# Half of the next block's transposed inputs loaded into the free columns of the row scales' buffer

## The chip, the cores and the metric

One core of a Trainium2 chip runs the whole program; 7 other cores of the chip are not used. The metric is the time of one execution on the device, in microseconds (us). Engines: TensorE (PE; its weight loads are PEld), VectorE (DVE), ScalarE (ACT), GpSimd (POOL); SyncE (SP) and POOL issue the DMAs.

## What is computed

One inference step of a one-layer streaming encoder: 2048 prompt frames and 64 sample frames of width 1024, all float32. Cut to what matters here:

```python
hn   = rms(x) * (1 + sc1) + sh1            # adaLN-modulated pre-norm
proj = hn @ w_in                           # q, f, iv, og (HGRN2), xr, gr (RG-LRU)
...
y = concat([o_hg, o_rg]) @ w_out
x = x + g1 * y
hn2 = rms(x) * (1 + sc2) + sh2
x = x + g2 * (square(relu(hn2 @ w_up)) @ w_down)   # D_FF = 4096
y_out = rms(x) * final_gain
```

## The kernel before

The prompt is cut into four blocks of 512 frames (`BLK`); the last block also carries the 64 sample frames. A block goes through the pre-norm (`phase_A`), the two mixers, the output projection (`phase_O`) and the MLP. The MLP runs over 8 groups `g` of 512 hidden columns. `phase_U(g)` multiplies by `w_up` (4 weight units, 96 matmuls of 512 columns) and squares the relu. `phase_W(g - 1)` multiplies the group before by `w_down`: 7 products instead of 8 (a Strassen-like scheme), 84 matmuls. In block 0 a plain product, `phase_D0` with 96 matmuls, stands in its place. After group 7's `phase_U` come `phase_W(6)` and `phase_W(7)`, and then the next block's projections. The stretch around the last three of these is called a **seam** here: seam 1 is from block 0 to 1, seam 2 from 1 to 2, seam 3 from 2 to 3.

Every weight is float32 and is used as a high part and a rest. `split_raw` casts a loaded `raw` tile on ACT (L244) and subtracts on DVE (L245) into a `wt` tile; the pool `wp` has 6 of them. `phase_W` first makes its 7 weights in `down_units`: two of the four loaded `w_down` units go to `raw` buffers (L250, 3 of them), two to row buffers (L1032 and L1033), then DVE combines them with four subtractions (L1036) and splits seven tiles. The products accumulate in PSUM, and DVE adds each to its accumulator (L1086; L1068 in block 0). For `phase_W(g)` itself the operand sums of `phase_U(g)` are made by `sums_of`: splits (L964 on ACT, L965 on DVE) and four additions (L970 to L974). 

The next block's pre-norm is begun inside the MLP of the block before. `phase_A1` (in group 5) computes the row scales. `phase_A` (in group 7) spreads them over 128 partitions with TensorE (`ps_rs`, L529), copies them to the first 512 columns of a buffer `hd_a` of 2560 columns (L531), and loads the block's input once more, transposed, in four tiles of 128 x 1024 (L501, `in_x_t`). Each tile gives two column groups: DVE multiplies by scale (L538), ACT writes the high part (L539), DVE the rest (L540): 16 DVE instructions a block. For the last block `phase_A` first norms the 64 sample frames over a buffer `hd_a` of their own (`norm_T`, L390 to L419).

Buffers of a tag are shared by all that asks for that tag:

- `xa`: 2 buffers. The first two tiles of the transposed input; the `x2r` tiles of the final phase, `phase_E` (L1180).
- `row`: 2 buffers of 1028 columns. **The last two tiles of the transposed input**, two of the four `w_down` units of every `phase_W`, the row vectors `final_gain` and `gscr` (L351), and earlier in a block temporaries of the RG-LRU.
- `hd`: 2 buffers of 2560 columns: `hd_u` of `phase_U`, `hd_a` of `phase_A`, `hd_h` of the heads.

The order of the work on each engine is made by the tile scheduler from priorities (`sec(block, rank)`) and from its own estimate of when buffers come free. Each engine, and SP's DMA queue too, then works its list off in order: what waits holds all that stands behind it.

```python
x = rowp.tile([P, 1028], F32, tag="row", name="x_a")[:, :D] if row else xap.tile([P, D], F32, tag="xa", name="x_a")   # L500
...
r12, r22 = (rowp.tile([P, 1028], F32, tag="row", name="raw")[:, :D] for _ in range(2))   # L1031, in down_units
Q.dma_start(r12, w_down[u + 2])   # L1032
```

Of the kernel before, what the change touches and what calls it, by code (L numbers as in the profile page):

```python
# [9 lines left out]
F32 = mybir.dt.float32  # L10
# [9 lines left out]
P = 128  # L20
D = 1024
# [108 lines left out]
def hymba_step(ctx: ExitStack, tc: tile.TileContext, i: dict, o: dict):  # L130
# [18 lines left out]
    def pool(name, bufs, **k):  # L149
        return ctx.enter_context(tc.tile_pool(name=name, bufs=bufs, **k))  # L150
# [8 lines left out]
    xap = pool("xap", 2)  # L159
    rowp = pool("rowp", 2)  # L160
# [216 lines left out]
    def rms_rstd(x, junk, n):  # L377
        ss = smp.tile([P, 8], F32, tag="ss", name="ss")
        S.activation(junk[:n], x[:n], AF.Square, accum_out=ss[:n, 0:1])
        V.tensor_scalar(ss[:n, 0:1], ss[:n, 0:1], 1.0 / D, EPS, op0=ALU.mult, op1=ALU.add)  # L380
        return rsqrt(ss, n, 1)

    def norm_T(xn, hn, XT, t0, n, which, psc, psh):

        hv = hn.rearrange("p (k t) -> p k t", t=P)
        for hf in range(2):
            ps = pax.tile([P, 512], F32, tag="ax", name="ps_T")
            for q in range(4):
                k = hf * 4 + q
                T.transpose(ps[:, q * P:q * P + n], xn[:n, k * P:(k + 1) * P], ident[:n, :n])  # L390
            for q in range(4):
                k = hf * 4 + q
                sc, sh = modc[:, psc, which, k:k + 1], modc[:, psh, which, k:k + 1]
                if q % 2:
                    V.tensor_scalar(hv[:, k, :n], ps[:, q * P:q * P + n], sc, sh, op0=ALU.mult, op1=ALU.add)
                else:
                    S.activation(hv[:, k, :n], ps[:, q * P:q * P + n], AF.Identity, scale=sc, bias=sh)
            ks = slice(hf * 4, hf * 4 + 4)
            S.copy(XT.p[0][:, ks, t0:t0 + n], hv[:, ks, :n])  # L399
            V.tensor_tensor(XT.p[1][:, ks, t0:t0 + n], hv[:, ks, :n], XT.p[0][:, ks, t0:t0 + n].bitcast(F32), op=ALU.subtract)  # L400
            if which:
                XT.pair(ks)
# [50 lines left out]
    for b in range(NB):  # L453
        B = Block()
# [38 lines left out]
    def gate(dma, ins):  # L493
        tc.add_manual_dep(dma.ins, ins.ins.name,
                          mybir.DependencyInfo(mybir.DependencyClass.Sync, mybir.DependencyReason.DATA),
                          reason="late load")


    def x_load(src, n, after, row=False):
        x = rowp.tile([P, 1028], F32, tag="row", name="x_a")[:, :D] if row else xap.tile([P, D], F32, tag="xa", name="x_a")  # L500
        d = Q.dma_start(x[:n], src)  # L501
        if after is not None:
            gate(d, after)
        return x

    def phase_A1(B, after=None):

        ss = smp.tile([P, 8], F32, tag="ss", name="ss_a")
        for t in range(4):
            x = x_load(xp[B.toks[t][4]:B.toks[t][4] + P], P, after)  # L510
            S.activation(x, x, AF.Square, accum_out=ss[:, t:t + 1])
        V.tensor_scalar(ss[:, 0:4], ss[:, 0:4], 1.0 / D, EPS, op0=ALU.mult, op1=ALU.add)
        B.rs = rsqrt(ss, P, 4)

    def phase_A(B, after=None):


        B.XT = Split(xtp, "xt", KD, "XT1")
        if B.last:
            n = LS  # L520
            x = x_load(xs, n, after)
            hd = hdp.tile([P, 2560], F32, tag="hd", name="hd_a")
            rs = rms_rstd(x, hd[:, :D], n)
            V.tensor_scalar(x[:n], x[:n], rs[:n, 0:1], None, op0=ALU.mult)
            norm_T(x, hd[:, 0:D], B.XT, BLK, n, 1, SC1, SH1)
        hd = hdp.tile([P, 2560], F32, tag="hd", name="hd_a")
        ps = pax.tile([P, 512], F32, tag="ax", name="ps_rs")
        for t in range(4):
            T.matmul(ps[:, t * P:(t + 1) * P], lhsT=B.rs[:, t:t + 1].to_broadcast([P, P]), rhs=ident, start=True, stop=True)  # L529
        rb = hd[:, 0:BLK]  # L530
        S.copy(rb, ps)  # L531
        for k2 in range(4):
            x = x_load(i["x_t"][B.b, k2], P, after, k2 > 1).rearrange("p (k t) -> p k t", k=2)
            for kk in range(2):
                k = 2 * k2 + kk
                sc, sh = modc[:, SC1, 0, k:k + 1], modc[:, SH1, 0, k:k + 1]
                hi, lo = (y[:, k, :BLK] for y in B.XT.p)
                V.scalar_tensor_tensor(x[:, kk], x[:, kk], sc, rb, op0=ALU.mult, op1=ALU.mult)  # L538
                S.activation(hi, x[:, kk], AF.Identity, bias=sh)  # L539
                V.scalar_tensor_tensor(lo, x[:, kk], sh, hi.bitcast(F32), op0=ALU.add, op1=ALU.subtract)  # L540
# [686 lines left out]
    if blocks[0].last:  # L1227
        run([ada_first(0)], 99)
        run(ada_s, 99)
        phase_A(blocks[0])  # L1230
    else:
        phase_A0(blocks[0])
# [4 lines left out]
    for B in blocks:  # L1237
# [48 lines left out]
        for g in range(NG):  # L1286
            if B.last and g == NG - 1:
                with sec(b, 177):
                    phase_W(B, g - 1, gts[g - 1])
                with sec(b, 178):  # L1290
                    combine(B)
            with sec(b, 110 + 10 * g):
                gts.append(phase_U(B, g))
            if g == 5 and not B.last:
                with sec(b, 161):
                    phase_A1(blocks[b + 1], B.ulast)
            if g == NG - 1 and not B.last:
                with sec(b, 182):
                    phase_A(blocks[b + 1])
            if g and not (B.last and g == NG - 1):  # L1300
                with sec(b, 115 + 10 * g):
                    (phase_W if b else phase_D0)(B, g - 1, gts[g - 1])
                with sec(b, 116 + 10 * g):
                    if b == 0 and g < 7:
                        run(ada_s, 11)
# [33 lines left out]
```

## Time and profile before

| | |
|---|---|
| median of 3 runs | 2690.6 us (2690.57 to 2698.39) |
| the profiled execution | 2700.03 us; span 2698.3 us, so 1.7 us lie around the span |
| mean granted clock of TensorE | 0.955 of full speed |
| PE busy | 2493.6 us, 92% of the span |
| DVE busy | 1817.2 us, 67% |
| ACT busy | 1043.5 us, 39% |
| POOL busy | 188.0 us, 7% |
| DMA | 397 MB, 147 GB/s on the mean |

A share of the span is a mean over stages with different limits. What the stages at the seams wait for stands in the timeline of instructions: there, "[13.81 <-ACT wt L244]" behind an instruction says that its engine stood idle for 13.81 us before it, and that the cast of line 244 ended the wait.

### The profile page before, as it was taken

To read this page: it belongs to the slowest core of one execution; us is meant where nothing else is said; L and a number is where in the kernel's file an instruction comes from. 1 tells how busy PE (TensorE), PEld (TensorE's weight loads), DVE (VectorE), ACT (ScalarE), POOL (GpSimd) and SP (SyncE) were. 2 spreads that over 40 slices of the span, in tenths; PEclk is the share of its full clock that TensorE was granted. 3 is DMA by queue.
4 is the path that set the end of the run, shared out by engine and by line. 5 is a ranking of instruction groups with operands and counts; after the bars stand their busy time and mean duration, and the time that the engine had idled before them with its cause. 6 is when DMAs were issued, how large, how long until landed. Compare 5 with 4: busy or idle time off the path is not lost.

```text
span 2698.3 us, 34804 instructions
## 1 busy us (share of the span) xinstructions
PE 2493.6 (92%) x13592; PEld 2129.3 (79%) x13592; DVE 1817.2 (67%) x3267; ACT 1043.5 (39%) x1683; POOL 188.0 (7%) x245
## 2 busy tenths in 40 slices
PE   5878899999899999999799989999789998999997
PEld 4866787887797778888587878888579877998976
DVE  7676675766554656878864656778773576568787
ACT  4234152223212446445312436445411624644432
POOL 2311100000011100000001100000010110000000
PEclk8888799999999999999899999999889999999998
DMA  8563555667353542234363442234253643222223
GB/s 332 219 227 132 202 182 187 211 210 242 126 203 124 180 141 78 94 110 156 113 223 125 180 140 79 94 109 153 93 207 110 149 126 129 79 78 92 81 68 109
DMA packets 96420, 397.44 MB, mean 147 GB/s; under 512 B 14432, under 2 KB 16384, under 8 KB 79360
## 3 DMA queue, kind: packets, MB, share of 16 engines
q1 hardware_dynamic: 79696, 274.63, 29.6%
q0 software_dynamic: 16560, 120.59, 12.9%
q8 instruction: 107, 1.75, 0.3%
q14 instruction: 57, 0.47, 0.0%
HBM read 343.77 MB, written 51.41 MB: 146 GB/s over the span
## 4 chain that ended last, share of the span: by engine, by line
PE 70%; DVE 14%; issue 7%; DMA 5%; ACT 3%; POOL 1%; SPq 0%; DVEq 0%; POOLq 0%; ACTq 0%
PE ps_u L1011 24%; PE ps_d L1097 15%; PE ps_in L649 7%; PE ps_vo L767 6%; PE ps_d L1063 6%; PE ps_y L937 3%; DMA raw<-in_w_ada_dram 2%; PE ps_lv L841 2%; DVE wt L245 2%; PE ps_in L634 1%; PE ps_rg L710 1%; DVE ada_acc L333 1%; PE ps_s L1107 1%; PE ps_ada L337 1%; DMA wt<-kept_out 1%
## 5 line engine op out<-in xcount | busy, mean ns | idle before, releaser
L1011 PE MATMUL ps_u<-XT,wt 128*128 128x512 f32 (+2 forms) x4128 | 746.5, 341 | 17.1 <-ACT XT L399 5.9
L1011 PEld LDWEIGHTS ps_u<-XT,wt 128*128 128x128 f32 x4128 | 656.0, 189 | 99.4 <-ACT XT L399 7.1
L245 DVE TENSOR_TENSOR wt<-raw,wt 128x1024 fp32r<-128x1024 f32 x338 | 414.9, 1240 | 237.6 <-ACT wt L244 206.1
L244 ACT CAST wt<-raw 128x1024 fp32r<-128x1024 f32 x357 | 371.4, 1048 | 331.4 <-PE ps_d L1063 93.1
L649 PE MATMUL ps_in<-XT,wt 128*128 128x512 f32 (+1 forms) x1776 | 377.7, 363 | 12.9 <-ACT wt L244 6.6
L649 PEld LDWEIGHTS ps_in<-XT,wt 128*128 128x128 f32 x1776 | 293.0, 191 | 60.3 <-ACT wt L244 8.5
L1097 PE MATMUL ps_d<-wt,gS 128*128 128x512 f32 x1104 | 269.0, 402 | 41.0 <-ACT wt L244 30.7
L1097 PEld LDWEIGHTS ps_d<-wt,gS 128*128 128x128 f32 x1104 | 212.8, 194 | 92.8 <-ACT wt L244 32.3
L937 PE MATMUL ps_y<-wt,mix 128*128 128x512 f32 x800 | 207.1, 413 | 13.6 <-DVE hd_o L942 5.1
L1014 ACT ACTIVATE hd_u<-ps_u 128x512 f32<-128x512 f32 (+2 forms) x172 | 85.2, 498 | 344.3 <-PE ps_u L1011 341.0
L767 PE MATMUL ps_vo<-wt,XT 128*128 128x256 f32 x1600 | 212.6, 289 | 2.6 <-POOL wt L245 1.7
L767 PEld LDWEIGHTS ps_vo<-wt,XT 128*128 128x128 f32 x1600 | 201.0, 195 | 3.9 <-POOL wt L245 1.9
L1097 PE MATMUL ps_d<-wt,gA 128*128 128x512 f32 x828 | 196.9, 390 | 0.2
L937 PEld LDWEIGHTS ps_y<-wt,mix 128*128 128x128 f32 x800 | 154.8, 198 | 53.0 <-DVE hd_o L942 6.4
L1063 PE MATMUL ps_d<-wt,gt 128*128 128x512 f32 x768 | 182.2, 398 | 8.3 <-DVE acc L1068 8.3
L1097 PEld LDWEIGHTS ps_d<-wt,gA 128*128 128x128 f32 x828 | 154.7, 188 | 33.0 <-DVE wt L245 1.0
L1063 PEld LDWEIGHTS ps_d<-wt,gt 128*128 128x128 f32 x768 | 147.9, 193 | 40.1 <-DVE acc L1068 8.7
L1036 DVE TENSOR_TENSOR raw<-raw 128x1024 f32<-128x1024 f32 x92 | 113.4, 1233 | 4.3 <-DMA raw<-in_w_down_dram 2.2
L841 PEld LDWEIGHTS ps_lv<-hd_h 128*128 128x128 f32 x640 | 88.9, 211 | 24.6 <-issue 15.6
L1086 DVE TENSOR_TENSOR acc<-acc,ps_d 128x512 f32<-128x512 f32 x160 | 106.5, 680 | 1.9 <-PE ps_d L1097 0.9
L841 PE MATMUL ps_lv<-hd_h 128*128 128x64 f32 x640 | 92.3, 292 | 14.5 <-DVE hd_h L846 9.0
L1086 DVE TENSOR_TENSOR accM<-accM,ps_d 128x512 f32<-128x512 f32 x120 | 79.7, 681 | 38.5 <-PE ps_d L1097 38.1
(306 smaller groups left out, 2671.1 us busy)
## 6 DMA issues: line engine op xcount, KB each, us to landing
wt<-kept_in POOLq DMA_DIRECT2D x72, 1024.0 KB, 6.8
raw<-in_w_up_dram SPq DMA_DIRECT2D x128, 512.0 KB, 4.3
raw<-in_w_down_dram SPq DMA_DIRECT2D x128, 512.0 KB, 3.5
raw<-in_w_ada_dram SPq DMA_DIRECT2D x80, 512.0 KB, 4.8
wt<-kept_out POOLq DMA_DIRECT2D x24, 1024.0 KB, 5.2
kept_in<-wt POOLq DMA_DIRECT2D x19, 1024.0 KB, 8.8
raw<-in_w_in_dram SPq DMA_DIRECT2D x24, 512.0 KB, 5.3
x_a<-in_x_prompt_dram SPq DMA_DIRECT2D x16, 512.0 KB, 5.3
```

What stands on the lines that cost most here:

```text
L244: S.copy(wt[:, 0], raw)
L245: eng.tensor_tensor(wt[:, 1], raw, wt[:, 0].bitcast(F32), op=ALU.subtract)
L649: T.matmul(ps[:, :pn], lhsT=w[:, a, k], rhs=B.XT.p[x][:, k, p0:p0 + pn], start=(k == 0 and q == 0), stop=(k == KD - 1 and q == 2))
L767: T.matmul(ps[:rows(B.toks[ti]), :256], lhsT=l, rhs=ws[k // 4][:, a, k % 4], start=(q == 0), stop=(q == len(ops) - 1))
L841: T.matmul(ps[:C, c * C // 2:(c + 1) * C // 2].rearrange("p (b h) -> p b h", h=hs), lhsT=KS[:, c * C:c * C + C], rhs=qv[:, c * bc:(c + 1) ...
L937: T.matmul(ps[:rows(B.toks[ti])], lhsT=l, rhs=ws[k - k % 2][:, a, k % 2], start=(q == 0), stop=(q == len(ops) - 1))
L1011: T.matmul(ps[:, :pn], lhsT=w[:, a, k], rhs=B.XT.p[x][:, k, p0:p0 + pn], start=(k == 0 and q == 0), stop=(k == KD - 1 and q == 2))
L1014: S.activation(r, ps[:, :pn], AF.Relu)
L1036: V.tensor_tensor(d, x, y, op=ALU.subtract)
L1063: T.matmul(ps, lhsT=l, rhs=ws[half][c // 2][:, a, c % 2], start=(q == 0), stop=(q == len(ops) - 1))
L1086: return V.tensor_tensor(dst, dst, ps, op=ALU.add)
L1097: T.matmul(ps, lhsT=op[x][y][:, c, t * P:(t + 1) * P], rhs=w[:, a, c], start=(k == 0), stop=(k == len(ops) - 1))
```

## The change

`x_load` takes the buffer as an argument instead of a flag. `phase_A` issues its four loads ahead of the copy of the row scales, and the last two tiles no longer take row buffers: they lie in columns 512 to 1535 and 1536 to 2559 of `hd_a`, whose first 512 columns hold the row scales as before.

```diff
-    def x_load(src, n, after, row=False):
-        x = rowp.tile([P, 1028], F32, tag="row", name="x_a")[:, :D] if row else xap.tile([P, D], F32, tag="xa", name="x_a")
+    def x_load(src, n, after, x=None):
+        if x is None:
+            x = xap.tile([P, D], F32, tag="xa", name="x_a")
         d = Q.dma_start(x[:n], src)
...
         rb = hd[:, 0:BLK]
+        xts = [x_load(i["x_t"][B.b, k2], P, after, hd[:, k2 * D - 1536:k2 * D - 512] if k2 > 1 else None) for k2 in range(4)]
         S.copy(rb, ps)
         for k2 in range(4):
-            x = x_load(i["x_t"][B.b, k2], P, after, k2 > 1).rearrange("p (k t) -> p k t", k=2)
+            x = xts[k2].rearrange("p (k t) -> p k t", k=2)
```

The number and the sizes of all instructions stay the same. Behind line 500 the changed file's lines are 1 higher, behind line 531 2 higher: its L1034 and L1035 are L1032 and L1033 of before, L1038 is L1036, L1088 is L1086, L540 and L542 are L538 and L540.

The list of SP's DMA queue at seam 2, before, from the first transposed loads on (two `x_a` are the tiles of tag `xa`, the next two those of tag `row`; L1032 and L1033 load `w_down` units to row buffers, first for group 6, then for group 7):

```order
L501 DMA x_a<-in_x_t_dram 128x1024 x2
L250 DMA raw<-in_w_up_dram 128x1024
L501 DMA x_a<-in_x_t_dram 128x1024 x2
L250 DMA raw<-in_w_up_dram 128x1024 x2
L250 DMA raw<-in_w_down_dram 128x1024 x3
L1032 DMA raw<-in_w_down_dram 128x1024
L1033 DMA raw<-in_w_down_dram 128x1024
L250 DMA raw<-in_w_down_dram 128x1024
```

and the same place in the change:

```order
L502 DMA x_a<-in_x_t_dram 128x1024 x2
L250 DMA raw<-in_w_up_dram 128x1024
L1034 DMA raw<-in_w_down_dram 128x1024
L1035 DMA raw<-in_w_down_dram 128x1024
L250 DMA raw<-in_w_up_dram 128x1024 x2
L250 DMA raw<-in_w_down_dram 128x1024 x3
L502 DMA hd_a<-in_x_t_dram 128x1024 x2
L250 DMA raw<-in_w_down_dram 128x1024
```

Group 6's two row-buffer loads and the last two transposed tiles have changed places.

The list of DVE at seam 2, before, from the splits during `phase_U(7)` on, through the beginning of `phase_A`'s 16 instructions (the 16 end thirteen rows further on, one row behind the first L1086; the first L1036 of group 6 comes two rows after them):

```order
L245 TENSOR_TENSOR wt<-raw,wt 128x1024 x5
L965 TENSOR_TENSOR gA_9562<-hd_u,gA_9562 128x512
L538 SCALAR_TENSOR_TENSOR x_a<-x_a,modc,hd_a 128x512 x3
L540 SCALAR_TENSOR_TENSOR XT_9587<-x_a,modc,XT_9587 128x512 x2
L965 TENSOR_TENSOR gA_9565<-hd_u,gA_9565 128x512
L540 SCALAR_TENSOR_TENSOR XT_9587<-x_a,modc,XT_9587 128x512
L538 SCALAR_TENSOR_TENSOR x_a<-x_a,modc,hd_a 128x512 x2
```

and in the change:

```order
L245 TENSOR_TENSOR wt<-raw,wt 128x1024 x4
L1038 TENSOR_TENSOR raw<-raw 128x1024
L245 TENSOR_TENSOR wt<-raw,wt 128x1024
L1038 TENSOR_TENSOR raw<-raw 128x1024
L245 TENSOR_TENSOR wt<-raw,wt 128x1024 x2
L967 TENSOR_TENSOR gA_9560<-hd_u,gA_9560 128x512
L1038 TENSOR_TENSOR raw<-raw 128x1024 x2
L245 TENSOR_TENSOR wt<-raw,wt 128x1024 x2
L540 SCALAR_TENSOR_TENSOR x_a<-x_a,modc,hd_a 128x512 x3
L542 SCALAR_TENSOR_TENSOR XT_9585<-x_a,modc,XT_9585 128x512
```

All four subtractions and four more splits of group 6's weights now stand ahead of `phase_A`'s first instruction. Where the 16 instructions end, the change has the last split of group 6 and then the first L1088:

```order
L245 TENSOR_TENSOR wt<-raw,wt 128x1024
L542 SCALAR_TENSOR_TENSOR XT_9585<-hd_a,modc,XT_9585 128x512
L1088 TENSOR_TENSOR accM<-accM,ps_d 128x512 x2
L1088 TENSOR_TENSOR acc<-acc,ps_d 128x512 x3
```

So the first addition from PSUM stands behind all 16 of them, as it stood behind 15 before.

At seam 3 (`hd_a` of L395 is the sample frames' buffer) the change's DVE list reads, from the first subtraction to the first of the 16:

```order
L1038 TENSOR_TENSOR raw<-raw 128x1024
L967 TENSOR_TENSOR gA_14160<-hd_u,gA_14160 128x512
L1038 TENSOR_TENSOR raw<-raw 128x1024
L245 TENSOR_TENSOR wt<-raw,wt 128x1024 x2
L1038 TENSOR_TENSOR raw<-raw 128x1024 x2
L245 TENSOR_TENSOR wt<-raw,wt 128x1024
L395 TENSOR_SCALAR hd_a<-ps_T,modc 128x64 x3
...
L245 TENSOR_TENSOR wt<-raw,wt 128x1024
L967 TENSOR_TENSOR gA_14163<-hd_u,gA_14163 128x512
L400 TENSOR_TENSOR XT_14185<-hd_a,XT_14185 128x4x64
L245 TENSOR_TENSOR wt<-raw,wt 128x1024
L540 SCALAR_TENSOR_TENSOR x_a<-x_a,modc,hd_a 128x512
```

Here nine of group 6's instructions (four subtractions, five splits) have come ahead, where before none of them stood between those rows. At seam 1, where `phase_D0` takes no row buffers, DVE's list is in the same order as before, and SP's two `hd_a` loads stand behind five `w_down` loads and the store of `gscr`, where the two row-buffer tiles stood among the first of those.

## Rows read from the trace of the kernel before

**Rows 1.** The page, chain that ended last: share of the span by engine.

```profile
PE 70%; DVE 14%; issue 7%; DMA 5%; ACT 3%; POOL 1%; SPq 0%; DVEq 0%; POOLq 0%; ACTq 0%
```

**Rows 2.** By stretch, seam 2: length; busy PE, PEld, DVE, ACT, POOL; clock; DMA share, GB/s.

```profile
1280.00:1300.00 20.00, 17.87 (x83) 14.60 (x81) 7.67 (x13) 9.25 (x15) 0.00 (x0) 1.00 0.00 1
1300.00:1320.00 20.00, 8.28 (x25) 6.16 (x26) 18.98 (x26) 6.85 (x9) 0.00 (x0) 0.58 0.23 79
1320.00:1340.00 20.00, 18.53 (x77) 13.81 (x76) 19.52 (x24) 6.77 (x9) 0.53 (x1) 1.00 0.50 171
```

**Rows 3.** Timeline of PE, seam 2: start, us, engine, instruction, [idle before <-releaser].

```profile
1269.58 21.92 PE L1011 MATMUL ps_u<-XT,wt 128*128 128x512 f32 x96
...
1292.15 5.72 PE L1097 MATMUL ps_d<-wt,gA 128*128 128x512 f32 x24
1311.68 12.51 PE L1097 MATMUL ps_d<-wt,gS 128*128 128x512 f32 x42 [13.81 <-ACT wt L244]
...
1356.53 11.04 PE L649 MATMUL ps_in<-XT,wt 128*128 128x512 f32 x48
...
1374.50 1.65 PE L820 MATMUL ps_dg<-hd_h 128*128 128x128 f32 x8 [3.10 <-POOL hd_h L816]
```

**Rows 4.** Timeline of all engines, seam 2.

```profile
1293.31 2.08 DVE L538 SCALAR_TENSOR_TENSOR x_a<-x_a,modc,hd_a 128x512 f32<-128x512 f32 x3 [10.00 <-ACT hd_a L531]
...
1305.66 0.33 SPq L1032 DMA_DIRECT2D raw<-in_w_down_dram  x1
...
1309.32 1.22 DVE L1036 TENSOR_TENSOR raw<-raw 128x1024 f32<-128x1024 f32 x1
...
1310.58 1.04 ACT L244 CAST wt<-raw 128x1024 fp32r<-128x1024 f32 x1 [2.87 <-DVE raw L1036]
```

**Rows 5.** Timeline of SP's queue, ahead of seam 2.

```profile
1250.32 3.96 SPq L501 DMA_DIRECT2D x_a<-in_x_t_dram  x2
```

**Rows 6.** Chain in order of time, seam 2: start, us, what.

```profile
1302.44 0.66 DVE x_a L538
...
1304.36 0.60 DVE hd_u L974
...
1309.41 1.15 DVE raw L1036
```

**Rows 7.** Timeline of all engines, seam 3.

```profile
1902.38 0.34 DVE L395 TENSOR_SCALAR hd_a<-ps_T,modc 128x64 f32<-128x64 f32 x1 [9.16 <-ACT hd_a L397]
1902.90 5.72 PE L1097 MATMUL ps_d<-wt,gA 128*128 128x512 f32 x24
...
1907.20 2.07 DVE L538 SCALAR_TENSOR_TENSOR x_a<-x_a,modc,hd_a 128x512 f32<-128x512 f32 x3
...
1923.12 1.22 DVE L1036 TENSOR_TENSOR raw<-raw 128x1024 f32<-128x1024 f32 x1 [1.03 <-DMA raw<-in_w_down_dram]
...
1925.47 1.65 PE L1097 MATMUL ps_d<-wt,gS 128*128 128x512 f32 x3 [16.86 <-ACT wt L244]
1925.55 1.22 DVE L1036 TENSOR_TENSOR raw<-raw 128x1024 f32<-128x1024 f32 x1 [1.21 <-DMA raw<-in_w_down_dram]
```

**Rows 8.** Timeline of PE, end of seam 3.

```profile
1970.61 9.68 PE L649 MATMUL ps_in<-XT,wt 128*128 128x288 f32 x72
...
1986.60 1.16 PE L820 MATMUL ps_dg<-hd_h 128*128 128x128 f32 x8 [2.36 <-POOL hd_h L816]
1991.03 1.97 PE L841 MATMUL ps_lv<-hd_h 128*128 128x64 f32 x8 [3.27 <-DVE hd_h L817]
```

**Rows 9.** Timelines of SP's queue and of all engines, seam 1.

```profile
678.25 0.29 SPq L346 DMA_DIRECT2D gscr<-grow  x1
...
701.24 0.74 DVE L538 SCALAR_TENSOR_TENSOR x_a<-x_a,modc,hd_a 128x512 f32<-128x512 f32 x1
...
712.51 12.70 PE L1063 MATMUL ps_d<-wt,gt 128*128 128x512 f32 x47 [8.25 <-DVE acc L1068]
```

**Rows 10.** The instructions on `in_x_t`, last line: from issue to landing.

```profile
DMA to landing us min/median/max: 3.5/3.6/5.2
```

## The prediction

> **What bounds the kernel now.** I read the chain of waits first: 70% of it is PE and 14% DVE [rows 1], so time is to be had only where PE stands still, and there it is mostly DVE that ends the wait. Then the busy time by stretch: PE is full in the steady groups and has its holes at the seams. At seam 2 it is busy 8.28 of 20 us, and DVE is then at 18.98 and 19.52 of 20, after only 7.67 in the 20 us before [rows 2]. So the seam is bound by DVE, right behind a stretch in which DVE had little to do.
>
> The timelines say why. A matmul of 512 columns takes 21.92 / 96 = 0.228 us in the steady state, so the 168 of `phase_W(6)` and `phase_W(7)` need 38.3 us; from 1292.15 to the next block's first matmul at 1356.53 they took 64.4 [rows 3]. The first 24 ran, then PE stood 13.81 us for a cast [rows 3], and that cast waited for a subtraction L1036 of `down_units` [rows 4]. The subtraction needs the unit of L1032, which SP issued only at 1305.66 [rows 4], because `phase_A`'s last two tiles had taken both row buffers at 1250 [rows 5] and gave them back only when DVE had used them. Meanwhile DVE had stood idle for 10.00 us ahead of `phase_A` [rows 4]. Seam 3 is alike: 16.86 us of PE, 9.16 us of idle DVE ahead of it, and twice more DVE waited for the late units, 1.03 and 1.21 us [rows 7]; from its first matmul at 1902.90 to the projections at 1970.61 it took 67.7 us [rows 7, 8]. At seam 1 PE waits 8.25 us for an addition that stands behind `phase_A` on DVE [rows 9]; no row buffer plays a part.
>
> **The change, part by part.** Nothing is added or removed: the same 12 loads of 512 KB, the same 48 DVE instructions on operands of the same shape, which I cost at nothing more. What changes is when things may start.
>
> *Seam 1.* Row buffers are free sooner, but DVE's and PE's lists there are the same. The two `hd_a` loads go past five `w_down` loads and the store of `gscr` on SP, which was issued at 678.25; a tile lands in at most 5.2 us [rows 10], well before the 701.24 at which `phase_A` begins [rows 9]. 0 us.
>
> *Seam 2.* SP now issues L1032 and L1033 where the row-buffer tiles stood, at 1250 [rows 5]; they land some 25 us before their use. By the new list DVE does four L1036 and four more L245 ahead of `phase_A`. Each holds DVE 1.15 us (the chain's piece [rows 6]), so 8 x 1.15 = 9.2 us of work goes from a stretch without slack into the 10.00 us of idling. Their buffers allow it: each further `wt` comes free when `phase_U(7)` ends a unit, every 5.5 us. The last of the eight waits for the fourth unit, and its cast (1.04 us [rows 4]) now stands on ACT ahead of the copy of the row scales, so `phase_A` begins at about 1294.3, 1.0 us later. DVE's list behind it ends 9.2 - 1.0 = **8.2 us** sooner, and I take that.
>
> It is not the whole stall, since what PE waits for is next the first L1086. PE can go 30 matmuls with the PSUM it has, then needs an addition, which stands behind 16 x 0.66 (`phase_A`), 6 x 0.60 (`sums_of`) [rows 6] and one split of 1.15: 15.3 us from 1294.3, at 1309.6 instead of the 1311.68 at which PE went on before. So I expect a stall of 10 to 11 us in place of 13.81, with another cause. The bounds: below, only what PE gains by that, 2.1 us and 6 more matmuls done, 1.4: 3.5 us. Above, PE without any wait from 1309.6: 138 x 0.228 = 31.5, ending at 1341.1, 15.4 us sooner. DVE's own sum lies between and DVE was without slack there, so I take 8.2.
>
> *Seam 3.* Nine instructions go ahead (four L1036, five L245): 10.3 us, seven of them into the 9.16 us of idling [rows 7]. DVE's waits for late units, 2.24 us [rows 7], go. Against that, `phase_A` begins later than 1907.20: by two splits less one addition that has gone behind (2.3 - 0.6), and one cast, 1.0, on ACT ahead of the copy: 2.7 us, at 1909.9; the addition gone behind costs 0.6 again. 10.3 + 2.2 - 2.7 - 0.6 = **9.2 us**. The first addition that PE then waits for comes 15 x 0.66 + 5 x 0.60 = 12.9 us on, at 1922.8, against 1925.47. Bounds as above: 2.7 + 1.4 = 4.1 us, and 1922.8 + 31.5 = 1954.3, 16.3 us sooner. Here the `hd_a` loads wait: their columns come free when the sample frames' norm is done, at about 1908.5. With a landing of 3.6 us (5.2 at most) [rows 10] they are there at 1912 to 1914, and DVE comes to the first of them after some 7 us of `phase_A`, at 1917. That cover is 3 us; each us beyond it would hold DVE, and PE with it. What stands right behind these loads on SP, a `w_up` unit of the next block and the first `x2r`, is not wanted at the seam.
>
> *Behind the seams.* The next block's first head waited 3.10 us at seam 2 [rows 3], and 2.36 and 3.27 at seam 3 [rows 8], for DVE work that stood behind `phase_E`'s additions of `x2r`, whose loads land late. In the new list L815 stands ahead of the third of these additions. Bounds 0 and 8.7 us; since parts of that head still stand behind them, I take half, **4 us**.
>
> The sum: 8.2 + 9.2 + 4 = 21.4 us off the profiled execution's 2700.03. That execution is 9.4 us above the median of the runs, 2690.6; against the median the forecast is **2669 us**.
>
> **The rivals.**
>
> *The stall only changes its cause.* DVE's list is shorter, but it then waits for PE here and there, and only the earlier restart is left: 3.5 + 4.1 = 7.6 us, 2683. For it: the first L1086 does stay behind all of `phase_A`. Against: DVE was idle for only 1.5 of the 40 us of the seam in rows 2 (20 - 18.98 and 20 - 19.52), so 9 us less work cannot all turn to idling.
>
> *The whole hole closes.* From the restart on PE runs without a wait: 15.4 + 16.3 + 8.7 = 40.4 us, 2650. Against: all 28 additions and all of `down_units(7)` still stand on DVE in those 31 us. The Trainium skill bears on this ("Perfetto Trace Analysis", Optimization Strategy): it reads gaps that repeat as a sign that too few buffers stop the next tile. By that rule the two largest gaps are the row buffers' alone and go with them; the trace agrees as to their cause, and the busy time of DVE right behind them speaks against their going whole.
>
> *Slower: the clock.* In the 20 us of seam 2's stall the granted clock was 0.58, then 1.00 again [rows 2]; the 42 matmuls behind the stall took 12.51 us where 9.6 would do at 0.228 [rows 3], so such a restart costs 2.9 us now. If PE's idling, now in more and shorter pieces, kept the clock at its lower level (half of full speed) through both `phase_W`, the 138 matmuls of a seam would take 31.5 us more, 63 for two, and the kernel 63 - 21 = 42 us longer: 2732. It turns slower from 94 such matmuls over both seams on. For it: a stall of some 10 us stays at each of the two seams. Against: after the stall of 13.81 us the clock was back at 1.00 in the next 20 us, though PE was busy in only 18.53 of them [rows 2]. The Trainium skill ("TensorE: Matmul & The Clock Gate", HAM oscillation) tells of a kernel whose clock fell anew at every gap and lost 26.7 of 211 us by it; by that rule the gaps that I leave would each cost a warm-up, and the seams' gain would shrink by what it costs. The row of 0.58 agrees that a gap lowers it, the row of 1.00 that one warm-up was enough.
>
> *It does nothing:* the loads of L1032 come early but the casts are held by `wt` tiles, 2691. Against: the list has only as many splits ahead as units of `phase_U(7)` end.
>
> **How the numbers follow.** Chances: the forecast with its bounds 0.72, the changed cause 0.12, the closed hole 0.08, slower by the clock (or by late `hd_a` loads at seam 3) 0.05, nothing 0.03. A measurement of this kernel can tell about 0.3%, 8 us, from no change. Faster by more: the forecast, the closed hole and a third of the changed cause, 0.84. Within it: 0.11. Slower: 0.05. The range leaves out the slower case, the closed hole's far end and the no-effect case: from 2659 (half way between what I take and the upper bounds, 21.4 and 40.4) to 2684 (both lower bounds).
>
> **What would show it.** In the profile of the change: L1034 issued near 1250 and DVE busy with L1038 during `phase_U(7)`; the waits of 13.81 and 16.86 us gone from the cast and a wait of 10 to 13 us for an addition (L1088) in their place; the projections 8 to 9 us sooner behind `ps_rs` at each seam; seam 1 as it was. Wrong if seam 1 moves, if DVE is idle for over 3 us in the 40 us from 1300 on, if `hd_a` loads end a DVE wait, or if the clock stays low behind the stall.

## The result and the profile after

| | before | after |
|---|---|---|
| median, first series | 2691.66 us (4 runs, 2690.57 to 2698.39) | 2676.39 us (4 runs, 2673.15 to 2676.63) |
| ratio, first series | | 0.9937, 95% interval 0.9921 to 0.9954 |
| median, second series | 2696.65 us (11 runs) | 2675.62 us (6 runs) |
| ratio, second series | | 0.9918, 0.9905 to 0.9931 |
| profiled execution | 2700.03 us | 2676.52 us (span 2674.7) |
| mean granted clock | 0.955 | 0.958 |
| PE busy / DVE busy | 2493.6 / 1817.2 us | 2492.6 / 1816.1 us |

It is faster by 0.6 to 0.8%: 15.3 us in the first series, 21.0 in the second (experiment 4). The work over the whole span is the same to about 1 us on PE and DVE; only idle time went.

The chain of waits by engine, on the page of after, is that of [rows 1] but for one point between "issue" and DMA:

```profile
PE 70%; DVE 14%; issue 6%; DMA 6%; ACT 3%; POOL 1%; SPq 0%; DVEq 0%; POOLq 0%; ACTq 0%
```

Seam 2, timeline of PE (start, us, instruction, idle before it and its releaser), which answers to [rows 3]:

```profile
1288.91 1.05 PE L530 MATMUL ps_rs<-ident,rsq 128*128 128x128 f32 x8
1289.72 5.72 PE L1099 MATMUL ps_d<-wt,gA 128*128 128x512 f32 x24
1295.28 1.52 PE L1099 MATMUL ps_d<-wt,gS 128*128 128x512 f32 x6
1307.90 11.49 PE L1099 MATMUL ps_d<-wt,gS 128*128 128x512 f32 x42 [11.10 <-DVE accM L1088]
...
1333.00 7.10 PE L1099 MATMUL ps_d<-wt,gS 128*128 128x512 f32 x30 [1.37 <-DVE acc L1088]
...
1342.66 2.66 PE L651 MATMUL ps_in<-XT,wt 128*128 128x512 f32 x11
```

The wait for a cast is gone, and one of 11.10 us for an addition L1088 stands in its place. From `ps_rs` to the first projection it is now 53.75 us, before 65.19. The timeline of DVE there, against [rows 4]:

```profile
1275.62 1.23 DVE L1038 TENSOR_TENSOR raw<-raw 128x1024 f32<-128x1024 f32 x1
...
1290.67 1.22 DVE L245 TENSOR_TENSOR wt<-raw,wt 128x1024 fp32r<-128x1024 f32 x1 [4.21 <-ACT wt L244]
1291.82 2.07 DVE L540 SCALAR_TENSOR_TENSOR x_a<-x_a,modc,hd_a 128x512 f32<-128x512 f32 x3
...
1307.17 1.27 DVE L1088 TENSOR_TENSOR accM<-accM,ps_d 128x512 f32<-128x512 f32 x2
```

The subtractions of group 6 begin at 1275, in the last `phase_U`, where before they began at 1309. `phase_A` starts at 1291.82, and the first addition at 1307.17, 0.7 us ahead of PE's restart: what PE waits for is that addition, behind all 16 instructions of `phase_A`. SP's queue shows why the subtractions could come early (before: [rows 5] and the L1032 of [rows 4]):

```profile
1248.58 0.33 SPq L1034 DMA_DIRECT2D raw<-in_w_down_dram  x1
1251.53 0.33 SPq L1035 DMA_DIRECT2D raw<-in_w_down_dram  x1
...
1271.85 0.90 SPq L502 DMA_DIRECT2D hd_a<-in_x_t_dram  x2
```

Seam 3, timeline of PE, against [rows 7, 8]: 57.84 us from `ps_rs` to the projections, before 68.63.

```profile
1886.28 1.16 PE L530 MATMUL ps_rs<-ident,rsq 128*128 128x128 f32 x8
...
1907.32 10.74 PE L1099 MATMUL ps_d<-wt,gS 128*128 128x512 f32 x36 [11.69 <-DVE accM L1088]
...
1933.02 8.54 PE L1099 MATMUL ps_d<-wt,gS 128*128 128x512 f32 x30 [2.70 <-DVE acc L1088]
...
1944.12 9.68 PE L651 MATMUL ps_in<-XT,wt 128*128 128x288 f32 x72
...
1960.46 2.08 PE L822 MATMUL ps_dg<-hd_h 128*128 128x128 f32 x8 [2.39 <-POOL hd_h L818]
1962.50 1.97 PE L843 MATMUL ps_lv<-hd_h 128*128 128x64 f32 x8
```

Where did 11.4 and 10.8 us come from? The busy time from `ps_rs` to the first projection tells it (length; busy PE, PEld, DVE, ACT, POOL; clock; DMA). Before, seams 2 and 3:

```profile
1291.34:1356.53 65.19, 46.29 (x178) 35.08 (x176) 60.61 (x80) 22.58 (x29) 2.64 (x5) 0.82 0.46 160
...
1901.98:1970.61 68.63, 46.65 (x179) 35.39 (x178) 62.90 (x86) 24.09 (x35) 1.85 (x4) 0.80 0.40 135
```

and after:

```profile
1288.91:1342.66 53.75, 41.28 (x178) 33.50 (x176) 51.41 (x71) 19.13 (x26) 2.64 (x5) 0.90 0.39 141
...
1886.28:1944.12 57.84, 43.45 (x179) 35.10 (x177) 53.88 (x77) 21.02 (x32) 2.79 (x4) 0.85 0.41 149
```

At seam 2 DVE has 60.61 - 51.41 = 9.2 us less work and 4.58 - 2.34 = 2.2 us less idling; at seam 3, 9.0 and 1.8. DVE's groups of instructions name the 9.2 us. Before, seam 2:

```profile
L245 DVE TENSOR_TENSOR wt<-raw,wt 128x1024 fp32r<-128x1024 f32 x12 | 14.2, 1217 | 0.5 <-ACT wt L244 0.5
...
L1036 DVE TENSOR_TENSOR raw<-raw 128x1024 f32<-128x1024 f32 x8 | 9.7, 1217 | 0.0
...
L1115 DVE TENSOR_TENSOR acc<-acc,accM 128x512 f32<-128x512 f32 x4 | 2.6, 680 | 0.0
...
L1115 DVE TENSOR_TENSOR acc<-acc 128x512 f32<-128x512 f32 x2 | 1.4, 682 | 0.0
```

and after:

```profile
L245 DVE TENSOR_TENSOR wt<-raw,wt 128x1024 fp32r<-128x1024 f32 x9 | 10.8, 1218 | 4.2 <-ACT wt L244 4.2
...
L1038 DVE TENSOR_TENSOR raw<-raw 128x1024 f32<-128x1024 f32 x4 | 4.9, 1218 | 0.0
...
L1117 DVE TENSOR_TENSOR acc<-acc,accM 128x512 f32<-128x512 f32 x3 | 2.1, 685 | 0.0
...
L1117 DVE TENSOR_TENSOR acc<-acc 128x512 f32<-128x512 f32 x1 | 0.7, 683 | 0.0
```

Four subtractions and three splits (8.0 us at 1.15) have left the seam, and two closing additions (L1117, 1.2 us) now lie behind the first projection, since PE's last product is done sooner.

### The profile page after: what moved, and what is told of

It reads as the page before. It is cut to its first block, busy times and chain, and to the rows that moved or that the text cites. A ratio compares the mean times of both kernels' runs of the same rounds, so it can differ in the third digit from the quotient of the medians.

```text
span 2674.7 us, 34794 instructions
## 1 busy us (share of the span) xinstructions
PE 2492.6 (93%) x13592; PEld 2135.7 (80%) x13592; DVE 1816.1 (68%) x3267; ACT 1042.9 (39%) x1683; POOL 187.1 (7%) x245
## 3 DMA queue, kind: packets, MB, share of 16 engines
HBM read 343.77 MB, written 51.41 MB: 148 GB/s over the span
## 4 chain that ended last, share of the span: by engine, by line
PE 70%; DVE 14%; issue 6%; DMA 6%; ACT 3%; POOL 1%; SPq 0%; DVEq 0%; POOLq 0%; ACTq 0%
PE ps_u L1013 24%; PE ps_d L1099 14%; PE ps_in L651 8%; PE ps_vo L769 7%; PE ps_d L1065 6%; DMA raw<-in_w_ada_dram 3%; PE ps_lv L843 2%; PE ps_y L939 2%; DVE wt L245 2%; PE ps_in L636 1%; PE ps_rg L712 1%; PE ps_s L1109 1%; DVE ada_acc L333 1%; DMA wt<-kept_out 1%; DVE ada_acc L288 1%
## 5 line engine op out<-in xcount | busy, mean ns | idle before, releaser
L651 PE MATMUL ps_in<-XT,wt 128*128 128x512 f32 (+1 forms) x1776 | 377.5, 363 | 13.3 <-ACT wt L244 6.6
L1099 PE MATMUL ps_d<-wt,gS 128*128 128x512 f32 x1104 | 261.8, 396 | 27.1 <-DVE accM L1088 22.8
L1038 DVE TENSOR_TENSOR raw<-raw 128x1024 f32<-128x1024 f32 x92 | 113.5, 1233 | 2.2
L1088 DVE TENSOR_TENSOR acc<-acc,ps_d 128x512 f32<-128x512 f32 x160 | 106.3, 680 | 1.7 <-PE ps_d L1099 0.6
L1088 DVE TENSOR_TENSOR accM<-accM,ps_d 128x512 f32<-128x512 f32 x120 | 79.9, 681 | 37.1 <-PE ps_d L1099 36.3
L843 PE MATMUL ps_lv<-hd_h 128*128 128x64 f32 x640 | 92.0, 291 | 13.7 <-DVE hd_h L848 10.9
```

What stands on the lines that cost most here:

```text
L651: T.matmul(ps[:, :pn], lhsT=w[:, a, k], rhs=B.XT.p[x][:, k, p0:p0 + pn], start=(k == 0 and q == 0), stop=(k == KD - 1 and q == 2))
L843: T.matmul(ps[:C, c * C // 2:(c + 1) * C // 2].rearrange("p (b h) -> p b h", h=hs), lhsT=KS[:, c * C:c * C + C], rhs=qv[:, c * bc:(c + 1) ...
L1038: V.tensor_tensor(d, x, y, op=ALU.subtract)
L1088: return V.tensor_tensor(dst, dst, ps, op=ALU.add)
L1099: T.matmul(ps, lhsT=op[x][y][:, c, t * P:(t + 1) * P], rhs=w[:, a, c], start=(k == 0), stop=(k == len(ops) - 1))
```

## The experiments

Two theories stood against each other once the change was seen. **DVE's sum**: a seam is as long as DVE's work in it, so only work that leaves the seam shortens it. **Order**: a seam is as long as it is because the first addition stands behind `phase_A` on DVE's list. Below, the length of a seam is taken from the end of the last `ps_u` matmul to the first `ps_in`, so that versions with `ps_rs` elsewhere compare: 55.25, 53.59 and 58.41 us in after; 54.59, 65.03 and 69.20 before.

The early issue of the loads with the row buffers kept was not run by itself for all blocks, but experiments 2 and 3 contain it in the blocks that keep them: their seams there are 65.8 us (seam 2) and 69.4 us (seam 3), against 65.0 and 69.2 before. So the gain is the buffers'. A third row buffer, which would part the two uses in another way, was not tried.

**1. The kernel before against itself.** No edit.

> The kernel before, unchanged, timed against itself: ratio 1.000, which shows how far two series of the same program differ. Its profile is a second execution of before. Seams (from ps_rs to the next block's first matmul): theory 'the two seams gave 22 us, the median shows 15 because the profiled execution of before lay 9 us over its median': ps_rs to ps_in again 65 us at seam 2 and 69 us at seam 3, and the 5 to 9 us of difference lie in stretches far from the seams. Rival 'the seams themselves vary from one execution to the next': one of the two is 3 us or more shorter here.

Ratio 1.0004 (0.9992 to 1.0017); its 12 runs lie between 2691.81 and 2706.03 us. The profile has seams of 55.0, 65.1 and 68.7 us: they repeat within 0.5 us, so the rival falls. Stretches between them vary more: from seam 2's first projection to the end of block 2's last `ps_u` it is 542.0 us, before 544.9. That 5 to 9 us lie in such stretches, as the first theory says, is not shown: both profiled executions of before took 2700 us.

**2 and 3. One seam at a time.** The row buffers are kept for all blocks but one (here block 2; the other run has block 3):

```diff
-        xts = [x_load(i["x_t"][B.b, k2], P, after, hd[:, k2 * D - 1536:k2 * D - 512] if k2 > 1 else None) for k2 in range(4)]
+        xts = [x_load(i["x_t"][B.b, k2], P, after, (hd[:, k2 * D - 1536:k2 * D - 512] if B.b == 2 else rowp.tile([P, 1028], F32, tag="row", name="x_a")[:, :D]) if k2 > 1 else None) for k2 in range(4)]
```

> Only block 2's last two transposed tiles (seam 2) lie in hd_a; the other blocks keep the row buffers. If the gain is made at each seam by itself: seam 2 falls from 65 to 54 us, seam 3 stays at 69, the time falls by 7 to 11 us (ratio 0.996 to 0.997). Rival 'the two seams share one gain, or the gain at a seam is lost again behind it': seam 2 falls, but the time falls by under 4 us.

> Only block 3's last two transposed tiles (seam 3) lie in hd_a. If the seams add up: seam 3 falls from 69 to 58 us, seam 2 stays at 65, the time falls by 7 to 11 us, and with the run of seam 2 alone the two sum to the 15 to 22 us of the whole change. Rival as there: under 4 us. If 2 to 3 us of the last block are lost by the change itself (longer landings of the transposed tiles, another order of the first heads), the stretch from the last block's first projection to the end is 730 us here as in the change, against 728 before.

| | seam 1 | seam 2 | seam 3 | ratio to before |
|---|---|---|---|---|
| seam 2 alone | 54.6 | 53.8 | 69.4 | 0.9958 (0.9943 to 0.9973) |
| seam 3 alone | 54.8 | 65.8 | 58.6 | 0.9947 (0.9930 to 0.9964) |

Each seam falls alone by what it falls in the whole change, and the other stays within 0.8 us. By the ratios the time falls by 11.3 and 14.3 us (10.3 and 12.6 between the medians), where the seams in the profiles fall by 11.3 and 10.6. The time agrees with the profiles within its intervals (4 and 5 us to each side). From the last block's first projection to PE's end it is 716.7 us with seam 3 changed, 715.9 without: no loss by the change shows there.

**4. The change again**, in one series with 5 to 7.

> The change itself once more, timed in one series with the three versions below. The two parts measured alone gave 11.3 us (seam 2) and 14.3 us (seam 3). If they add up and nothing is lost behind the seams: 20 to 25 us below before (ratio 0.991 to 0.993). Rival 'the first series was right, 7 us are lost again elsewhere': 15 us (ratio 0.9943). Seams in the profile as in the first execution: 55, 53.7 and 57.8 us.

Ratio 0.9918, 21.0 us between the medians; seams of 54.8, 53.7 and 58.4 us. The seams add up. The smaller 15.3 us of the first series go with a lower median of before there (2691.66 us of four runs, here 2696.65 of eleven), while that of the change is within 0.8 us; why it was lower is open.

**5. `phase_A` later.** One number:

```diff
-                with sec(b, 182):
+                with sec(b, 188):
                     phase_A(blocks[b + 1])
```

> The change, with phase_A at a rank behind phase_W(6) (188 in place of 182): the first L1088 no longer stands behind its 16 DVE instructions, but DVE has the same work. Theory 'order': PE's 11 us wait goes at all three seams and each gets 8 to 10 us shorter, the time 25 us below the change. Theory 'DVE's sum': DVE is busy 51.4 of the 53.75 us of seam 2 and 53.9 of the 57.8 us of seam 3, so there the 11 us wait is only spread over later waits, and seams 2 and 3 get shorter by 0 to 3 us (what the clock and the idling leave); at seam 1, where DVE is busy some 30 of 55 us, the order does count and the seam gets 8 to 10 us shorter. In all 8 to 14 us below the change.

2659.77 us, 15.9 us below the change. Seams 2 and 3: 53.6 and 57.2 us, so 0.1 and 1.2 us shorter than in experiment 4. Timeline of PE, seam 2, and the busy time of that seam:

```profile
1298.86 5.73 PE L1099 MATMUL ps_d<-wt,gA 128*128 128x512 f32 x24
1312.78 1.22 PE L1099 MATMUL ps_d<-wt,gS 128*128 128x512 f32 x2 [8.19 <-ACT wt L244]
...
1322.96 7.09 PE L1099 MATMUL ps_d<-wt,gS 128*128 128x512 f32 x30 [2.54 <-DVE acc L1088]
...
1332.61 1.75 PE L651 MATMUL ps_in<-XT,wt 128*128 128x512 f32 x7
```

```profile
1279.05:1332.61 53.56, 42.47 (x176) 33.53 (x176) 51.78 (x72) 19.67 (x26) 2.64 (x5) 0.90 0.43 152
```

The 11 us wait went, and one of 8.19 us for a weight of the next group came: its subtractions and splits stand among and behind `phase_A`'s instructions now. DVE is busy 51.78 of 53.56 us, as in the change. "Order" falls at seams 2 and 3, "DVE's sum" holds. At seam 1, where DVE has slack, order counts: 24 of the next block's matmuls are done inside the seam there, so it is read with the stretch behind it, from the end of block 0's last `ps_u` to that of block 1's: 584.0 us against 593.6 in experiment 4, 9.6 us less, within the 8 to 10 expected. The time fell by more than the 8 to 14 us expected in all; the two profiled executions differ by 11.8 us, of which these three places make 10.9.

**6. Part of `phase_A` ahead of the seam**, for blocks 1 and 2, then for all three. `ps_rs`, the four loads and the copy of the row scales go to `phase_P`, the eight multiplies to `phase_P2`; `phase_A` keeps the high parts and the rests:

```diff
+    def phase_P2(B):
+        for k in range(8):
+            x, kk = B.pre[k // 2], k % 2
+            V.scalar_tensor_tensor(x[:, kk], x[:, kk], modc[:, SC1, 0, k:k + 1], B.rb, op0=ALU.mult, op1=ALU.mult)
...
+                    with sec(b, 179.9):
+                        phase_P(N)
+                    with sec(b, 180.3):
+                        phase_P2(N)
                 with sec(b, 182):
-                    phase_A(blocks[b + 1])
+                    phase_A(N)
```

For block 3 the sample frames' normed rows go to the `ada` buffer, which is free there, and are also made at 179.85; only their writes to `XT` stay in `phase_A`.

> The change, and for blocks 1 and 2 phase_A is split: the ps_rs matmuls, the copy of the row scales, and the eight scale multiplies (L540) stand ahead of or inside the last phase_U, where DVE idles; only the high parts (ACT) and the rests (L542) stay behind it. Theory 'after the change the seam is bound by DVE's list, since the first L1088 stands behind all 16 instructions of phase_A': eight of the 16, 8 x 0.66 = 5.3 us, leave the list, so PE's wait for L1088 falls from 11.1 to about 6 us at seam 2 and its wait at seam 1 from 8.25 to about 3, and the time falls by 8 to 10 us against the change (2666 to 2668 us). Rival 'PE then waits for the next thing (a unit of w_down that lands late, a cast)': the waits move, and the time falls by under 4 us. Rival 'the multiplies hold up the splits of phase_U(7)': new waits of PE for casts inside phase_U(7), no gain.

> The split of phase_A at all three seams: as in the split before, and at seam 3 the sample frames' norm goes to a free buffer of its own, ahead of the last phase_U, so that the eight scale multiplies can go there too. Theory 'DVE's sum': seam 3 gets 5.3 us shorter for the multiplies and some 3 us for the norm's DVE work, 50 us in place of 58.3; seams 1 and 2 stay at 46.8 and 50.0. The time 8 us below the split of two seams, 2658 us where that has 2666. Rival: PE waits for the norm's transposes inside phase_U(7), seam 3 gains under 3 us.

| | seam 1 | seam 2 | seam 3 | median |
|---|---|---|---|---|
| split of two | 46.8 | 50.0 | 58.3 | 2665.96 us, ratio 0.9885 (0.9869 to 0.9901) |
| split of three | 46.8 | 50.2 | 51.7 | 2660.06 us, ratio 0.9862 (0.9844 to 0.9879) |

PE's waits for the first addition fell as DVE's list did, from 8.25 to 3.08 at seam 1 and from 11.10 to 5.05 at seam 2. Timeline of PE in the split of two, and the busy time of its seam 2:

```profile
709.89 38.42 PE L1076 MATMUL ps_d<-wt,gt 128*128 128x512 f32 x168 [3.08 <-DVE acc L1081]
...
1300.85 10.74 PE L1110 MATMUL ps_d<-wt,gS 128*128 128x512 f32 x36 [5.05 <-DVE accM L1099]
```

```profile
1287.64:1337.60 49.96, 42.29 (x168) 34.00 (x168) 47.48 (x65) 18.28 (x25) 2.64 (x5) 0.90 0.52 186
```

Two sizes were missed. Seam 2 got only 3.6 us shorter: PE's second wait grew from 1.37 to 2.62 us. DVE's sum says the same: from the end of `ps_u` on, DVE did 51.41 us of work there in the change and 47.48 in the split, 3.9 less. Eight multiplies had left (5.3 us at 0.66), but one split more (1.15 us) stands in the seam. Seam 1 got 8.5 us shorter, 3.3 more than its wait: `ps_rs` had left it (0.8 us), and the clock no longer fell. Busy time of seam 1 by stretch, the change:

```profile
705.00:710.00 5.00, 0.98 (x2) 0.83 (x3) 5.00 (x9) 2.16 (x3) 0.00 (x0) 0.50 0.39 140
710.00:715.00 5.00, 5.00 (x15) 3.93 (x14) 0.77 (x2) 0.00 (x0) 0.00 (x0) 0.58 0.02 3
```

and the split:

```profile
705.00:710.00 5.00, 1.92 (x9) 1.26 (x9) 5.00 (x9) 3.36 (x5) 0.00 (x0) 1.00 0.62 202
710.00:715.00 5.00, 5.00 (x22) 4.11 (x23) 2.25 (x3) 0.66 (x1) 0.00 (x0) 1.00 0.87 324
```

Behind the shorter wait the clock is 1.00 and 22 matmuls run in 5 us, where it was 0.58 and 15. The 168 matmuls behind the wait took 38.42 us instead of 40.79. In the split of three, seam 3 got 6.6 us shorter, not the 8.3 expected.

**7. Both:** the split of three, with what is left of `phase_A` at rank 188; run twice, the second time beside experiment 8.

> The split at three seams, and what is left of phase_A (eight high parts on ACT, eight rests on DVE) at a rank behind phase_W(6). DVE's work in seams 2 and 3 is now some 46 us, PE's 41 us at the full clock. Theory 'DVE's sum': 0 to 3 us per seam, from a clock that no longer falls. Theory 'order': PE's waits of 3, 5 and some 6 us at the three seams go, 10 to 14 us in all.

> The split at three seams with the rest of phase_A late, once more, beside the version with POOL: ratio to before 0.983 as in its first series, seams of 43.4, 49.1 and 49.7 us.

2652.75 and 2653.15 us, ratios 0.9834 (0.9817 to 0.9851) and 0.9830 (0.9811 to 0.9848): 22.9 us below the change in the same series, **faster than both kernels**. Seams of 43.4, 49.1 and 49.7 us; the second time 43.4, 47.4 and 49.5, so that seam 2 of one and the same program differs by 1.6 us between two executions. At seam 1, where DVE has slack, order counts: its 3.08 us wait is gone and it got 3.4 us shorter, and PE waits nowhere any more (43.4 us for 192 matmuls, 0.226 us each). Seams 2 and 3 got 1.2 to 2.8 and 2.0 to 2.2 us shorter, within the 0 to 3 us of the sum; there DVE is busy nearly throughout, here in the second run:

```profile
1282.04:1329.46 47.42, 41.27 (x168) 33.10 (x168) 46.28 (x63) 18.19 (x25) 2.65 (x5) 0.93 0.50 177
1872.87:1922.41 49.54, 42.40 (x169) 34.01 (x168) 47.29 (x66) 18.81 (x27) 2.45 (x5) 0.90 0.42 148
```

The Trainium skill ("Perfetto Trace Analysis", Optimization Strategy) says that where the most contended engine changes from one stretch to the next, interleaving the stretches can help. The trace agrees: the multiplies came out of a stretch in which DVE is the bound (46.28 of 47.42 us at seam 2 now) and went into the last `phase_U`, where PE is busy all the time and DVE had room (15.5 of 21.9 us ahead of seam 2 in the change, 19.1 of 22.0 now).

**8. Four of the eight rests on POOL.**

```diff
+                G.tensor_scalar(x[:, kk], x[:, kk], sh, None, op0=ALU.add)
+                G.tensor_tensor(lo, x[:, kk], hi.bitcast(F32), op=ALU.subtract)
...
-                V.scalar_tensor_tensor(lo, x[:, kk], sh, hi.bitcast(F32), op0=ALU.add, op1=ALU.subtract)
```

The edit also puts these four rests, with their high parts on ACT, back at rank 182; only DVE's four stay at 188.

> As the split at three seams with the rest of phase_A late, and four of the eight rests of each block are made on POOL (an addition and a subtraction, about 1.07 and 1.24 us by POOL's other instructions of that size) instead of DVE: 4 x 0.67 = 2.7 us of DVE less per seam. Theory 'DVE's sum' (DVE was busy 46.4 of 49.1 and 47.7 of 49.7 us of seams 2 and 3): each of the two gets some 2.5 us shorter, seam 1 (43.4 us, no wait left) stays, the time 5 us below the version without POOL. Rival 'POOL and DVE hinder each other': DVE's instructions of the seam get longer than 0.68 and 1.22 us while POOL works, and nothing is gained.

2665.63 us, 12.5 us above the same version without POOL; seams of 44.1, 49.7 and 50.7 us. Timelines of POOL and of DVE, seam 2:

```profile
1291.20 3.06 POOL L553 TENSOR_SCALAR hd_a<-hd_a,modc 128x512 f32<-128x512 f32 x1
1294.34 1.29 POOL L554 TENSOR_TENSOR XT<-hd_a,XT 128x512 fp32r<-128x512 f32 x1
```

```profile
1293.42 0.68 DVE L1011 TENSOR_TENSOR hd_u<-hd_u 128x512 f32<-128x512 f32 x1
1294.03 0.67 DVE L1127 TENSOR_TENSOR acc<-acc,ps_d 128x512 f32<-128x512 f32 x1
1294.62 1.55 DVE L1013 TENSOR_TENSOR hd_u<-hd_u 128x512 f32<-128x512 f32 x1
1296.10 0.68 DVE L1127 TENSOR_TENSOR acc<-acc,ps_d 128x512 f32<-128x512 f32 x1
```

The rival holds at the seams: an addition of two SBUF operands, 0.68 us elsewhere, took 1.55 while POOL's L554 worked, and DVE was busy 48.18 us at seam 2 with 62 instructions, against 46.28 with 63 without POOL. Additions from PSUM kept their 0.67 us. The Trainium skill ("SBUF — State Buffer", SBUF: two separate sides) tells of a port pair that a DVE instruction with two SBUF inputs and one of POOL hold in turn, each for its whole length; by that rule only DVE's instructions with two SBUF operands would lengthen, or POOL would wait for them. These rows agree with both: beside POOL's L553 the addition L1011 kept its 0.68 us, and it was L553 that took 3.06 (1.56 at the least).

The seams do not explain the loss: they are 0.7, 2.3 and 1.2 us longer than in experiment 7's second run, and seam 2 only 0.6 longer than in its first. From the last block's first projection to PE's end it is 730.2 us against 716.9. These 13.3 us lie ahead of that block's first `ps_u` (318.8 us behind the projection against 305.1), behind the last of the new POOL instructions at 1896.7; and the profiled execution, at 2675.53 us, was the slowest of the four. What made that stretch longer is open, so the 12.5 us are not shown to be the price of POOL's work beside DVE.

## Why the prediction was right, and where its steps were off

The sign and the mechanism came out: a wait for the first addition in place of the one for the cast, and a gain that goes by DVE's work. That the sum of 21.4 us met the 21.0 of the larger series is luck in part: the two seams were booked with 17.4 us and gave 22.2, and the 4 us behind them did not come. In the first series, with 15.3 us, the sum was too large. Step by step:

- **Seam 1: 0.** Right: 55.25 and 54.8 us against 54.6 and 55.0, with the same 8.25 us wait [rows 9].
- **Seam 2: 8.2 us, measured 11.4.** The mechanism was right: 30 matmuls, then a wait for L1088 of 11.10 us (10 to 11 said), restart 19.0 us behind `ps_rs` (18.3 said), `phase_A` 0.9 us later (1.0 said). The term was mis-sized where the text took DVE's own sum because DVE "was without slack there". It had some: 4.58 us of idling in the 65 us, and 2.34 are left; 2.2 us of the gain are that. Before, PE restarted at a lower clock (mean 0.86 from its restart to the projections, now 0.95), and DVE waited for it now and then. Another 1.2 us are the two closing additions that fell behind the first projection; the remaining 8.0 are the seven subtractions and splits. That idling and closing additions went because PE finished sooner is read from the rows, not tried alone.
- **Seam 3: 9.2 us, measured 10.8.** The same: 9.0 us less work, 1.8 less idling. The restart was said for 23.5 - 2.7 = 20.8 us behind `ps_rs` and came at 21.0. The `hd_a` loads were issued 6.2 us behind `ps_rs` (6.5 said). Their landing was said too short; against [rows 10], the loads of `in_x_t` in after:

```profile
DMA to landing us min/median/max: 5.3/5.7/6.5
```

  DVE's first instruction on them came 8.8 us behind the issue, so some 2 us of the cover were left, and no DVE wait was for them.
- **Behind the seams: 4 us, measured none.** From seam 2's first projection to block 2's last `ps_u` it is 541.5 to 544.9 us in three executions without the change there and 543.0 to 543.2 in three with it; from seam 3's projections to PE's end 715.9 to 719.3 and 716.6 to 719.3. The waits did shrink: the 3.27 us ahead of `ps_lv` [rows 8] are gone. But time did not follow: the first `ps_u` of the last block comes 306.0 us behind its first projection, against 305.2 before. The step that failed is to book a wait inside the mixers as time without naming what ends that stage; what ends that stage stays open.
- **The forecast of 2669 us** is 7 us below both medians of after. The sum did not do this (22.2 us at the seams against 21.4); the level did, from which it was taken. 2690.6 us was the median of three runs; over the later series before's median was 2696.8, 2696.7 and 2701.2 us, and 2697 - 21.4 is 2675.6.

Of the signs, DVE was idle for 0.6 us in the 40 us from 1300 on (39.42 busy), no `hd_a` load ended a DVE wait, and the projections came 11.4 and 10.8 us sooner behind `ps_rs` where 8 to 9 were said.

The rivals: "the stall only changes its cause" had the right picture of the wait, and failed on the gain, 22 us instead of 7.6. "The whole hole closes" failed on DVE's sum: a wait of 11 us is left at each of the two seams. "Slower: the clock" did not come: behind seam 2's restart the clock was 0.65 from 1308 to 1313 and 1.00 in the next 5 us. "It does nothing" fell with the subtractions at 1275.

## What to carry to other kernels

Where a wait is released by a buffer, find out what the engine behind it does in that stretch: count its busy time there by line, before and after. If it is full, the wait's length is no estimate of the gain; what leaves the stretch is. Reordering inside a full stretch gave little (experiment 5: 0.1 and 1.2 us at seams 2 and 3). Moving work to a stretch where the same engine idles gave its length less what came back in its place (experiment 6, seam 2: 3.6 us, with 3.9 less for DVE to do), and where the shorter wait spared the clock, more (seam 1). The level of the runs from which a gain is subtracted has an error of its own: three runs were 6 us off here.

## What was not expected of the hardware

With a wait of 3.08 us PE's granted clock stayed at 1.00 (the upper of its two levels; 0.50 is the lower, and what lies between is the mean of a stretch that holds both). One of 5.05 us came with 0.59 in the 5 us around its end (1298 to 1303 in the split of two) and 0.72 in the next 5. One of 8.25 us came with 0.50 and 0.58. So 5.2 us of wait saved were worth 7.5 at seam 1, where the 168 matmuls behind it took 2.4 us less; the rows are of one execution each. And POOL, nearly idle at the seams, was no free helper for DVE there: its twelve additions L553 took 1.56 to 3.06 us beside DVE, where the expectation had reckoned with 1.07 from another instruction, and some of DVE's lengthened.
